# One encoder layer on one core: all queues issued in the sequence of one list schedule

## The chip, the cores and the metric

The kernel runs on one core of a Trainium2 chip. The core has a matrix engine (TensorE, PE in the profile, with its weight loads as PEld), VectorE (DVE), ScalarE (ACT), GpSimd (POOL), SyncE (SP), which here only issues transfers, and DMA queues that move data between device memory and the on-chip memory. Each engine works through its own queue of instructions; an instruction that needs something of another queue waits for a semaphore. Matmuls write to PSUM, here eight tiles of 128x512 fp32, four named `mm` and four named `ax`.

The metric is device time in microseconds, the median of several executions. One more execution was taken with the hardware profiler on; every row of a profile in this document comes from such an execution.

## The reference

One layer of a hybrid encoder, sequence 512, width 1024, batch 1, all in fp32:

```python
h = _rmsnorm(x, norm_mix[i])
proj = h @ w_in[i]                                   # 768 q-latent | 256 kv-latent | 32 rope key | 3 x 512 Hyena
c_q, c_kv, k_pe, u_h = proj[..., :c1], proj[..., c1:c2], proj[..., c2:c3], proj[..., c3:]
q  = (_rmsnorm(c_q, q_norm[i]) @ w_uq[i])            # 8 heads x 96
kv = (_rmsnorm(c_kv, kv_norm[i]) @ w_ukv[i])         # 8 heads x (64 key + 64 value)
# q, k: rmsnorm per head, rotary on the last 32; softmax attention over 512 keys
y_attn = _block_attention(q, k, v)
u_h = _dwconv3(u_h, short_conv_w[i], short_conv_b[i]); x0, x1, vh = jnp.split(u_h, 3, axis=-1)
h_fwd, h_bwd = _hyena_filters(...)                   # three sine layers
y_hyena = x0 * _bidir_long_conv(x1 * vh, h_fwd, h_bwd, hyena_bias[i])   # FFT convolution
x = x + concat(_rmsnorm(y_attn), _rmsnorm(y_hyena)) @ w_out[i]
up = _dwconv3(_rmsnorm(x, norm_ffn[i]) @ w_up[i], ffn_conv_w[i], ffn_conv_b[i])
x = x + (jax.nn.silu(up[..., :D_FF]) * up[..., D_FF:]) @ w_down[i]      # D_FF = 2816
x = x + jax.nn.sigmoid(x @ w_ple_gate[i]) * _rmsnorm(p[i] @ w_ple[i], ple_norm[i])
```

## The kernel before

Everything is held transposed: a tile is 128 channels by 512 positions. Every fp32 operand of a large product is split into a high and a low part of a shorter format (`split`, lines 129 to 135), and each product of a 128x128 weight block with a 128x512 tile is three matmuls: high times high, high times low, low times high (`prod3`, line 181). A group of such matmuls that sums into one PSUM tile (8 blocks, 24 matmuls, for a 1024-deep product) is called a chain here.

Weights come as a stream of 115 tiles (`stream`, lines 149 to 156). `wload` (lines 137 to 147) loads one into `wr` (two buffers), writes the high part `wh` on ACT (line 142; three buffers) and the low part `wl` on DVE (line 143; three buffers); for the tiles of the first stages half of `wl` is made by ACT and an adding transfer on POOL's queue (lines 145, 146).

The stages, in the order in which TensorE takes them:

- The input projection, 21 weight tiles (`in_gemm`): first the two kv tiles together, then the rope key, twelve Hyena tiles and six q tiles. The sum of squares of x goes through `rms_bcast` (lines 218 to 222: a matmul with a tile of ones, then logarithm and exponential on ACT and two steps on DVE) into `R1`, by which each result is multiplied when it leaves PSUM. Between its matmuls, tasks of the filter network, the Fourier transforms and the spectral product are woven in (`spawn`, `advance`, with delays in constants such as `D_FILT`).
- Keys, queries, values, head norms and the inverse transforms. `query_scale` (line 674) sums squares with a ones matmul, copies the rows (`rows`, line 667, ACT), turns them by small transposes (`turn_rows`, line 231). `key_task` (lines 686 on) does the same for the keys, spreads the result (line 698 to 705, `t8`, `selT`), scales the keys, and calls `prep`, which moves one head's query and key rows by four transfers (lines 745, 746) and splits them (747, 748).
- Attention, head by head: scores (three matmuls on a 96-row operand), softmax (lines 864 to 869: maximum on DVE, exponential on ACT, division on POOL or DVE), turning of the probabilities (line 941), weighing (`weigh`), with the gates of the Hyena branch and the first part of the output projection between them.
- The output projection, then the up projection (44 tiles; each result goes through DVE line 1059, ACT 536, DVE 537 and 543, then SiLU, product and split), the down projection (eight chains of 66 matmuls, three weight tiles each), and the gate (eight tiles).

What sets the order: TensorE's queue follows the program's text (`manual_schedule(engines={PE})`). The other queues are sequenced by the framework's own scheduler, which the kernel steers by priorities (`high_priority` with offsets in `PRI`, `WPRI`, `CPRI`). Of the first head's four transfers all are issued from ACT's queue (`QACT = 1`), of the others from SP's.

Of the kernel before, what the change touches and what calls it, by code (L numbers as in the profile page):

```python
# [12 lines left out]
F32 = mybir.dt.float32  # L13
# [49 lines left out]
CPRI = 50  # L63
EPS = 1e-6
NH = 8
NFF = 22
# [17 lines left out]


@with_exitstack
def tile_encoder_block(
# [5 lines left out]
    nc = tc.nc  # L93
    V, S, G, PE, SP = nc.vector, nc.scalar, nc.gpsimd, nc.tensor, nc.sync

# [6 lines left out]
    def pri(key):  # L102
        return tc.high_priority(offset=PRI[key]) if PRI.get(key) else nullcontext()

    ctx.enter_context(tc.manual_schedule(engines={mybir.EngineType.PE}))
    const = ctx.enter_context(tc.tile_pool(name="const", bufs=1))
    apool = ctx.enter_context(tc.tile_pool(name="apool", bufs=16))
    wpool = ctx.enter_context(tc.tile_pool(name="wpool", bufs=2))
    gpool = ctx.enter_context(tc.tile_pool(name="gpool", bufs=20))
    xpool = ctx.enter_context(tc.tile_pool(name="xpool", bufs=8))  # L110
    psm = ctx.enter_context(tc.tile_pool(name="psm", bufs=4, space=PSUM))
    psx = ctx.enter_context(tc.tile_pool(name="psx", bufs=4, space=PSUM))

# [128 lines left out]

    def act_table(name):
        tc.keep_in_program_order(S.preload_act_table_set(name))

    act_table("natural_log_exp_and_others")


    p2 = ExitStack()
    hp = p2.enter_context(tc.tile_pool(name="hp", bufs=1))  # L250
    gp = p2.enter_context(tc.tile_pool(name="gp", bufs=1))
    p0 = ExitStack()
    ft = p0.enter_context(tc.tile_pool(name="ft", bufs=1, reuse_waits="tile"))

# [241 lines left out]
    rms_bcast(R1, accx, 1024, tmp, "x")  # L496
    SP.dma_start(rope, c_rope)
    SP.dma_start(ident, c_id)
    with tc.issue_after(gate_consts.ins):
# [6 lines left out]
        G.memset(f32(t8), 0.0)  # L506
    ckv = [xpool.tile([P, T], F32, tag="x", name="x") for _ in range(2)]
    for i in range(2):
# [141 lines left out]

    act_table("natural_log_exp_and_others")

# [79 lines left out]
    def prep(h, pool=None):  # L732
        j, i, g4, i4 = h // 2, h % 2, h // 4, h % 4
        raws = None if pool else {nm: atile(F32)[0:96, :] for nm in "qk"}
        for nm, src in (("q", qt), ("k", kt_)):
            if pool is None:
                raw = raws[nm]
                a, b = (atile()[0:96, :] for _ in range(2))
            else:
                raw = pool.tile([P, T], F32, tag=f"{nm}r", name=f"{nm}r")[0:96, :]  # L740
                ab = pool.tile([P, 2, T], F32R, tag=f"{nm}s", name=f"{nm}s")
                a, b = ab[0:96, 0, :], ab[0:96, 1, :]
            with tc.high_priority(offset=CPRI if h < 2 else 0):
# [148 lines left out]
    Rh = const.tile([P, T], F32, tag="R1", name="Rh")  # L892
    p0.close()


    p1 = ExitStack()
    at = p1.enter_context(tc.tile_pool(name="at", bufs=1, reuse_waits="tile"))

# [11 lines left out]
    Ra = at.tile([P, T], F32, tag="Ra", name="Ra")  # L910
    ap_ = p1.enter_context(tc.tile_pool(name="ap", bufs=1, reuse_waits="tile"))

# [89 lines left out]
    while fill < 8:  # L1002
        if fill == 8 - RFILL:
            with tc.high_priority(offset=RPRI):
                rms_bcast(Ra, acc5, 512, tmp1, "a")
# [32 lines left out]
    rms_bcast(R2, acc6, 1024, tmp1, "f")  # L1038
    p1.close()
    p2.close()  # L1040


    fp = ctx.enter_context(tc.tile_pool(name="fp", bufs=1, reuse_waits="tile"))

# [69 lines left out]
    for m in range(8):  # L1114
# [5 lines left out]
        if m == 0:  # L1120
            act_table("natural_log_exp_and_others")
# [177 lines left out]
```

## Time and profile before

| | us |
|---|---|
| median of 3 runs | 759.44 (757.58 to 759.54) |
| profiled execution, device time | 757.62 |
| its span, first to last instruction | 755.8 |
| TensorE busy | 723.0 |
| VectorE busy | 504.8 |
| ScalarE busy | 373.1 |
| GpSimd busy | 151.7 |

A row of a timeline gives start and duration in us, engine, line, operation, output<-inputs, sizes and how many equal instructions were merged; in brackets stands the idle time of the engine before it and what ended it. `PE` rows of merged matmuls overlap, so the distance between starts is the rate. A row of the windows gives, for one stretch, its length and then the busy time of each engine with its number of instructions, the granted TensorE clock as a share, the share of the DMA engines and GB/s. A row of waits gives who waited for whom, the total in us, how often, and the longest.

### The profile page before, as it was taken

The page shows a single profiled execution, that of the slowest core. Times are in us where ns is not written, and L with a number is a line of the kernel's source. Part 1 is how long each engine was busy: PE and PEld are TensorE (multiplying, and loading weights), DVE is VectorE, ACT ScalarE, POOL GpSimd, SP SyncE. Part 2 cuts the span into 40 slices and gives each one's busy share as a digit, 9 for nine tenths or more (in the row PEclk, how much of TensorE's full clock was granted, in tenths as well). Part 3 has the DMA queues.
Part 4 walks back from the last instruction along what each step waited for, and adds up shares of the span by engine and source line. Part 5 has one row for each costly group of instructions (what it writes and reads, how often), then busy time and mean ns, then how long its engine had stood idle before and what let it go on. Part 6 is the DMA issues. An engine that isn't in the chain of part 4 may idle for free.

```text
span 755.8 us, 9037 instructions
## 1 busy us (share of the span) xinstructions
PE 723.0 (96%) x3254; PEld 582.7 (77%) x3254; DVE 504.8 (67%) x780; ACT 373.1 (49%) x575; POOL 151.7 (20%) x150
## 2 busy tenths in 40 slices
PE   6999999996997899999999999999999999999997
PEld 4767888874665777788888888888888888888886
DVE  6499988888779987885766566666665332233482
ACT  7465545467668896564534444444353222126340
POOL 2111101110126662130422222222122000005000
PEclk9999999997999999999999999999999999999999
DMA  8765744443636210533232323232323233323331
GB/s 279 239 153 128 191 128 91 106 94 77 147 91 170 71 25 19 126 103 106 83 113 84 112 84 112 83 104 92 106 89 92 82 109 101 98 90 127 111 112 56
DMA packets 30110, 82.83 MB, mean 110 GB/s; under 512 B 3913, under 2 KB 5257, under 8 KB 30066
## 3 DMA queue, kind: packets, MB, share of 16 engines
q1 hardware_dynamic: 24418, 71.62, 31.2%
q0 software_dynamic: 5392, 10.25, 7.2%
q10 hardware_dynamic: 256, 0.39, 0.2%
q8 instruction: 25, 0.41, 0.2%
q14 instruction: 19, 0.16, 0.1%
HBM read 77.00 MB, written 2.10 MB: 105 GB/s over the span
## 4 chain that ended last, share of the span: by engine, by line
PE 54%; DVE 0%; ACT 0%; DVEq 0%; issue 0%
PE mm L176 37%; PE ax L176 17%; PE ax L220 0%; DVE t L1127 0%; ACT t L1126 0%; DVEq L1294 0%; DVE t L1128 0%
## 5 line engine op out<-in xcount | busy, mean ns | idle before, releaser
L176 PE MATMUL mm<-a,wh 128*128 128x512 f32 (+1 forms) x928 | 288.8, 392 | 9.2 <-ACT wh L273 6.4
L176 PEld LDWEIGHTS mm<-a,wh 128*128 128x128 f32 x928 | 174.3, 190 | 51.2 <-issue 6.5
L143 DVE TENSOR_TENSOR wl<-wr,wh 128x1024 fp32r<-128x1024 f32 (+3 forms) x113 | 124.3, 1101 | 113.8 <-ACT wh L142 111.8
L142 ACT ACTIVATE wh<-wr 128x1024 fp32r<-128x1024 f32 (+1 forms) x113 | 116.5, 1031 | 158.0 <-PE mm L176 121.6
L176 PE MATMUL mm<-a,wl 128*128 128x512 f32 (+1 forms) x464 | 180.7, 389 | 0.0
L176 PE MATMUL ax<-a,wh 128*128 128x512 f32 x384 | 118.3, 389 | 0.0
L176 PEld LDWEIGHTS mm<-a,wl 128*128 128x128 f32 x464 | 88.1, 190 | 17.8 <-DVE wl L274 0.2
L176 PEld LDWEIGHTS ax<-a,wh 128*128 128x128 f32 x384 | 72.1, 188 | 14.9
L176 PE MATMUL mm<-g,wh 128*128 128x512 f32 x232 | 73.8, 400 | 1.7 <-ACT t L647 1.7
L176 PE MATMUL ax<-a,wl 128*128 128x512 f32 x192 | 74.7, 389 | 0.0
L1063 POOL TENSOR_TENSOR f<-f 128x512 f32<-128x512 f32 x22 | 28.7, 1303 | 169.2 <-DVE f L543 149.5
L176 PE MATMUL mm<-h,wh 128*128 128x512 f32 x192 | 59.0, 389 | 0.0
L176 PEld LDWEIGHTS mm<-g,wh 128*128 128x128 f32 x232 | 44.2, 192 | 13.7 <-ACT t L647 2.1
L176 PE MATMUL mm<-g,wl 128*128 128x512 f32 x116 | 46.1, 397 | 0.0
L176 PEld LDWEIGHTS ax<-a,wl 128*128 128x128 f32 x192 | 36.0, 188 | 7.6
L176 PEld LDWEIGHTS mm<-h,wh 128*128 128x128 f32 x192 | 36.0, 188 | 7.5
L1059 DVE TENSOR_TENSOR f<-mm,R 128x512 f32<-128x512 f32 x22 | 15.2, 691 | 33.7 <-PE mm L176 33.7
L176 PE MATMUL mm<-h,wl 128*128 128x512 f32 x96 | 37.3, 389 | 0.0
L1062 ACT ACTIVATE f<-f 128x512 f32<-128x512 f32 x22 | 13.9, 631 | 44.8 <-DVE f L543 44.8
L536 ACT ACTIVATE f<-f,par 128x512 f32<-128x512 f32 x44 | 35.5, 808 | 1.0 <-DVE f L1059 1.0
L543 DVE SCALAR_TENSOR_TENSOR f<-f,par 128x511 f32<-128x511 f32 x44 | 33.9, 771 | 1.4
L146 POOL DMA_DIRECT2D wl<-in_w_in_dram x16 | 13.9, 868 | 103.8 <-DVE wl L143 53.5
(312 smaller groups left out, 1015.1 us busy)
## 6 DMA issues: line engine op xcount, KB each, us to landing
wr<-in_w_up_dram SPq DMA_DIRECT2D x44, 512.0 KB, 3.5
wr<-in_w_in_dram SPq DMA_DIRECT2D x19, 512.0 KB, 3.9
wr<-in_w_down_dram SPq DMA_DIRECT2D x16, 512.0 KB, 3.5
x<-in_xT_dram SPq DMA_DIRECT2D x16, 256.0 KB, 4.2
wl<-in_w_in_dram POOLq DMA_DIRECT2D x16, 256.0 KB, 5.3
wr<-in_w_out_dram SPq DMA_DIRECT2D x8, 512.0 KB, 4.4
wr<-in_w_gate_dram SPq DMA_DIRECT2D x8, 512.0 KB, 3.6
wr<-in_w_down_dram SPq DMA_DIRECT2D x8, 384.0 KB, 3.1
```

The lines of the kernel that those rows point to most:

```text
L142: S.activation(hi[:, :n], raw[:, :n], AF.Copy)
L143: V.tensor_tensor(lo[:, :cut], raw[:, :cut], f32(hi[:, :cut]), op=ALU.subtract)
L146: G.dma_start(lo[:, cut:n], src[:, cut:n], accum_op=ALU.add)
L176: last = PE.matmul(out, l, r, start=start and i == 0, stop=stop and i == n - 1)
L536: S.activation(c, z, AF.Identity, scale=pcol(w, 3 * m + 1), bias=pcol(b, m))
L543: V.scalar_tensor_tensor(c[:, 0 : T - 1], z[:, 1:T], pcol(w, 3 * m + 2), c[:, 0 : T - 1], op0=ALU.mult, op1=ALU.add)
L1059: V.tensor_tensor(z, ps_up.pop(m), R2, op=ALU.mult)
L1062: S.activation(cc[0], cc[0], AF.Silu)
L1063: G.tensor_tensor(cc[1], cc[0], cc[1], op=ALU.mult)
```

## The change

The kernel's text now calls recorders in place of the engines. Each call is kept as an operation with the parts of tiles that it reads and writes; from these follow its predecessors. Tiles are planned too: a pool's tag has numbered slots, taken in the program's order. `cost` gives each operation a duration and a latency by formulas of its engine and size. `order` gives TensorE's operations due times by the program's text (backward over the graph for everything else, and over TensorE's chains too), and then takes operations one after the other: for each engine the one that can start first, and of those within 0.02 of it the one that is due first. TensorE takes part in this, so its order may leave that of the text as well. `issue` emits the operations in that sequence, and the framework schedules nothing (`manual_schedule(engines=None)`). The priorities go away, and `QACT` is 0, so that the first head's four transfers are issued from SP's queue like those of the other heads. What is computed, and which engine computes it, stays.

```diff
-QACT = 1
+QACT = 0
...
+    def record(self, eng, fn, args, kw):
...
+        for views, write in ((ins, False), (outs, True)):
+            for v in views:
...
+                for other, obox, owrite in t.log:
+                    if other is not op and (write or owrite):
+                        if box[0] <= obox[1] and obox[0] <= box[1] and box[2] <= obox[3] and obox[2] <= box[3]:
+                            op.preds.add(other)
...
+    def cost(self, op):
...
+            else:
+                op.dur = (n + 32) / 2400.0
+            op.lat = 0.25
...
+    def order(self):
+        clock = 5.5
+        for op in self.ops:
+            if op.eng == "PE":
+                op.due = clock
+                clock += op.dur
+            else:
+                op.due = None
+            for p in op.preds:
+                p.succs.append(op)
+        for op in reversed(self.ops):
+            need = clock + 50.0 if op.due is None else op.due
+            for s in op.succs:
+                need = min(need, s.due - op.dur - op.lat - AIM - (2.0 + op.byte / 2.0e5 if op.byte else 0.0))
+            op.due = need
...
+                    for op in cand:
+                        t = max(op.est, engines[e])
+                        if op.port:
+                            t = max(t, port["G" if e == "V" else "V"])
...
+                    now = min(t for t, _ in fit)
+                    t, op = min(((t, op) for t, op in fit if t <= now + 0.02), key=lambda x: (x[1].due, x[1].i))
+                    if best is None or t < best[0]:
+                        best = (t, op)
...
+                engines[op.eng] = t + dur
+                op.end = t + dur + op.lat
...
+    def issue(self):
...
+        for _, op in self.order():
...
+            getattr(self.handles[op.eng], op.fn)(*[real(v) for v in op.args], **{k: real(v) for k, v in op.kw.items()})
...
-    V, S, G, PE, SP = nc.vector, nc.scalar, nc.gpsimd, nc.tensor, nc.sync
+    plan = Plan(tc, {"V": nc.vector, "S": nc.scalar, "G": nc.gpsimd, "PE": nc.tensor, "SP": nc.sync})
+    V, S, G, PE, SP = (plan.engine(k) for k in ("V", "S", "G", "PE", "SP"))
...
-    ctx.enter_context(tc.manual_schedule(engines={mybir.EngineType.PE}))
...
+    ctx.enter_context(tc.manual_schedule(engines=None))
...
-            with tc.high_priority(offset=WPRI if len(ready) > 3 else 0):
+            with nullcontext():
                 ready.append(wload(*stream[len(ready)]))
...
+    plan.issue()
```

Three places show what moves. In the rows `mm` and `ax` are PSUM tiles, `a` and `g` split activations, `wh` and `wl` the two parts of a weight tile; the last number of a name tells tiles apart, and in the changed kernel the number before it is the slot. All rows of the changed kernel have the line of `issue`.

TensorE near the start, before: the ones matmul that begins the first norm (`accx`) stands behind the whole chain of the third weight tile (`wh_203`, the rope key), that is behind 72 matmuls.

```order
L176 MATMUL mm_288<-a_160,wh_203 128x512
L176 MATMUL mm_288<-a_159,wl_204 128x512
L220 MATMUL ax_313<-accx_182,ones_81 128x512
L176 MATMUL mm_353<-a_125,wh_209 128x512
L176 MATMUL mm_353<-a_126,wh_209 128x512
```

TensorE at the same place in the changed kernel:

```order
L441 MATMUL mm_1_158<-a_15_234,wh_1_151 128x512
L441 MATMUL mm_1_158<-a_14_214,wl_1_160 128x512
L441 MATMUL ax_0_259<-accx_0_108,ones_0_88 128x512
L441 MATMUL mm_2_265<-a_0_113,wh_2_250 128x512
L441 MATMUL mm_2_265<-a_1_120,wh_2_250 128x512
```

It now stands right behind the two kv chains, 48 matmuls from the start; the rope key's chain (`mm_2_265`) follows it.

TensorE at the queries' scale, before: the four small transposes of the copied rows (`ident_80,t_1627`) stand directly behind those of `R1`.

```order
L176 MATMUL mm_1647<-g_1324,wh_1562 128x512
L176 MATMUL mm_1647<-g_1323,wl_1563 128x512
L231 MATMUL ax_1662<-ident_80,R1_189 128x8 x4
L231 MATMUL ax_1668<-ident_80,t_1627 128x8 x4
L690 MATMUL ax_1440<-qr_185,ones_81 8x512
L176 MATMUL mm_1647<-g_1375,wh_1562 128x512
```

TensorE at the same transposes (`t_9_1691`) in the changed kernel:

```order
L441 MATMUL mm_0_1598<-g_13_1445,wh_1_1530 128x512
L441 MATMUL mm_1_1653<-g_1_1289,wh_2_1567 128x512
L441 MATMUL mm_0_1598<-g_16_1427,wl_1_1540 128x512
L441 MATMUL ax_1_1696<-ident_0_238,t_9_1691 128x8 x4
L441 MATMUL mm_1_1653<-g_6_1277,wl_2_1573 128x512
L441 MATMUL mm_1_1653<-g_8_1350,wh_2_1567 128x512
```

Between the ones matmul of the queries' sum and these transposes stand 16 matmuls on 512 columns before, and the transposes of `R1`; in the changed kernel 46 matmuls on 512 columns, and the transposes of `R1` are spread among them.

TensorE in the up projection, before: one chain of 24 after the other, each on its own weight tile.

```order
L176 MATMUL ax_4051<-a_3344,wh_3967 128x512
L176 MATMUL ax_4051<-a_3343,wl_3968 128x512
L176 MATMUL mm_4094<-a_3177,wh_4010 128x512
L176 MATMUL mm_4094<-a_3178,wh_4010 128x512
L176 MATMUL mm_4094<-a_3177,wl_4011 128x512
```

TensorE in the up projection in the changed kernel:

```order
L441 MATMUL mm_3_3964<-a_7_3312,wh_2_3928 128x512
L441 MATMUL ax_0_4006<-a_9_3218,wh_0_3966 128x512
L441 MATMUL mm_3_3964<-a_6_3324,wh_2_3928 128x512
L441 MATMUL ax_0_4006<-a_10_3203,wl_0_3977 128x512
L441 MATMUL mm_3_3964<-a_7_3312,wl_2_3937 128x512
L441 MATMUL ax_0_4006<-a_11_3222,wh_0_3966 128x512
```

Two chains are open at a time nearly everywhere and take turns, matmul by matmul, so two of the three weight slots are in use together. Between the last matmul on a slot's old `wh` and the first on its new one stood 49 other matmuls before; now it is 25 in the up projection, and at nine places of the down projection and the last gate tile only 7. Further up, from the key scales' transposes (`ks`, line 698) to the first matmul that spreads them (`selT`, line 705), stood 24 matmuls on 512 columns before and stand four now. TensorE's queue changes its PSUM tile about 2,600 times in the changed kernel, and some 290 times before.

More of the change, by code (lines that the diff above doesn't have):

```diff
@@ L83, with _axes, _rearrange @@
 PI_LO = 3.1415925
+def _axes(side):
+    out, group = [], None
+    for w in side.replace("(", " ( ").replace(")", " ) ").split():
+        if w == "(":
+            group = []
+        elif w == ")":
+            out.append(group)
+            group = None
+        elif group is None:
+            out.append([w])
+        else:
+            group.append(w)
+    return out
+def _rearrange(idx, pattern, sizes):
+    left, right = (_axes(s) for s in pattern.split("->"))
+    size = dict(sizes)
+    for n, group in zip(idx.shape, left):
+        known = 1
+        for w in group:
+            known *= size.get(w, 1)
+        for w in group:
+            if w not in size:
+                size[w] = n // known
+    flat = [w for g in left for w in g]
+    idx = idx.reshape([size[w] for w in flat])
+    idx = idx.transpose([flat.index(w) for g in right for w in g])
+    shape = []
+    for g in right:
+        n = 1
+        for w in g:
+            n *= size[w]
+        shape.append(n)
+    return idx.reshape(shape)
@@ new lines, with __init__, shape, __getitem__ @@
+class View:
+    def __init__(self, tile, idx, steps, dtype):
+        self.tile, self.idx, self.steps, self.dtype = tile, idx, steps, dtype
+        self._box = None
+    @property
+    def shape(self):
+        return self.idx.shape
+    def __getitem__(self, key):
+        return View(self.tile, self.idx[key], self.steps + (("get", key),), self.dtype)
+    def rearrange(self, pattern, **sizes):
+        return View(self.tile, _rearrange(self.idx, pattern, sizes), self.steps + (("re", pattern, sizes),), self.dtype)
+    def bitcast(self, dtype):
+        return View(self.tile, self.idx, self.steps + (("cast", dtype),), dtype)
+    def box(self):
+        if self._box is None:
+            n = self.tile.width
+            row = self.idx[0]
+            self._box = (int(self.idx.min()) // n, int(self.idx.max()) // n, int(row.min()) % n, int(row.max()) % n)
+        return self._box
+    def real(self):
+        ap = self.tile.real
+        for s in self.steps:
+            if s[0] == "get":
+                ap = ap[s[1]]
+            elif s[0] == "re":
+                ap = ap.rearrange(s[1], **s[2])
+            else:
+                ap = ap.bitcast(s[1])
+        return ap
@@ new lines, with __init__, open_slots, view @@
+class Slot:
+    def __init__(self, pool, tag, n):
+        self.pool, self.tag, self.n = pool, tag, n
+        self.free = 0.0
+class Tag:
+    def __init__(self, pool, name, bufs):
+        self.pool, self.name, self.bufs = pool, name, bufs
+        self.tiles, self.next, self.slots = [], 0, None
+    def open_slots(self):
+        if self.slots is None:
+            self.slots = [Slot(self.pool, self, n) for n in range(min(self.bufs, len(self.tiles)))]
+        return self.slots
+class PlannedTile:
+    def __init__(self, tag, shape, dtype):
+        self.tag, self.shape, self.dtype = tag, tuple(shape), dtype
+        self.width = 1
+        for n in shape[1:]:
+            self.width *= n
+        self.slot, self.left, self.first, self.end, self.real = None, 0, None, 0.0, None
+        self.log = []
+    def view(self):
+        return View(self, np.arange(self.shape[0] * self.width, dtype=np.int32).reshape(self.shape), (), self.dtype)
@@ new lines, with __init__, tile @@
+class PlanPool:
+    def __init__(self, plan, name, bufs, kw):
+        self.plan, self.name, self.bufs, self.kw = plan, name, bufs, kw
+        self.first, self.last, self.tags = len(plan.cuts), None, {}
+        self.psum = kw.get("space") == PSUM
+        plan.pools.append(self)
+    def tile(self, shape, dtype, tag, name=None, bufs=None):
+        t = self.tags.get(tag)
+        if t is None:
+            t = self.tags[tag] = Tag(self, tag, bufs or self.bufs)
+        return PlannedTile(t, shape, dtype).view()
@@ new lines, with __init__, __getattr__ @@
+class Op:
+    __slots__ = ("i", "eng", "fn", "args", "kw", "acc", "seg", "preds", "succs", "dur", "lat", "due", "wait", "est", "new", "end", "table", "byte", "port")
+class Recorder:
+    def __init__(self, plan, eng, handle):
+        self._plan, self._eng, self._handle = plan, eng, handle
+    def __getattr__(self, fn):
+        return lambda *args, **kw: self._plan.record(self._eng, fn, args, kw)
+TABLES = {AF.Ln: "exp", AF.Exp: "exp", AF.Sin: "sin", AF.Silu: "silu", AF.Sigmoid: "sigmoid"}
@@ L241, in rms_cols @@
             rsqrt(out, v, col(), ps, n, "c")
[L243 to L253, printed above, removed]
+    nc.scalar.preload_act_table_set("natural_log_exp_and_others")
+    hp = plan.pool("hp", 1)
+    gp = plan.pool("gp", 1)
+    ft = plan.pool("ft", 1, reuse_waits="tile")
     def tmp(dt=F32):
@@ L496, in tile_encoder_block @@
     rms_bcast(R1, accx, 1024, tmp, "x")
-    SP.dma_start(rope, c_rope)
-    SP.dma_start(ident, c_id)
-    with tc.issue_after(gate_consts.ins):
+    plan.behind = gate_consts
+    if True:
+        SP.dma_start(rope, c_rope)
+        SP.dma_start(ident, c_id)
         for i in (0, 1):
@@ L506, in tile_encoder_block @@
         G.memset(f32(t8), 0.0)
+    plan.behind = None
     ckv = [xpool.tile([P, T], F32, tag="x", name="x") for _ in range(2)]
```

214 lines of the change are left out of this document (195 added, 19 removed).

## The prediction

> **What bounds the kernel now.** I first read the stretches, cut where the PE waits below end.
>
> ```profile
> span 755.8 us, 9037 instructions
> 0.00:40.00 40.00, 31.24 (x113) 23.71 (x114) 22.81 (x33) 23.80 (x36) 7.54 (x16) 0.96 0.82 256
> 40.00:150.00 110.00, 109.11 (x477) 87.39 (x477) 99.01 (x169) 55.73 (x81) 12.97 (x15) 1.00 0.54 133
> 150.00:214.60 64.60, 56.33 (x227) 38.31 (x225) 50.75 (x96) 42.66 (x79) 7.79 (x9) 0.92 0.47 111
> 214.60:300.00 85.40, 75.77 (x442) 61.68 (x442) 76.09 (x178) 67.84 (x144) 46.28 (x51) 1.00 0.28 69
> 340.20:751.20 411.00, 410.84 (x1830) 340.29 (x1830) 219.68 (x255) 159.61 (x203) 67.81 (x51) 1.00 0.31 98
> ```
>
> From 340 to 751 us TensorE is never idle, and the other engines are at half load or less: nothing is to be had there, only lost. The chain of waits says the same, matmuls one behind the other, and nothing else, up to 751 us:
>
> ```profile
> 352.78 5.44 PE ax L176 x24
> ...
> 712.69 38.42 PE mm L176 x192
> ```
>
> A matmul on 512 columns costs 5.44/24 = 0.227 us. All that the change can win lies before 340 us, in PE's waits:
>
> ```profile
> PE ax L231 <- ACT t L667: 6.5, 2, 5.8
> PE mm L176 <- ACT wh L273: 6.4, 1, 6.4
> PE ax L176 <- DVE ptl L132: 3.2, 2, 2.9
> PE mm L176 <- DVE x L509: 1.9, 1, 1.9
> PE mm L176 <- ACT t L647: 1.7, 1, 1.7
> PE mm L176 <- DVE ptl L132: 1.5, 5, 0.4
> PE ax L941 <- DVE st L865: 1.4, 1, 1.4
> PE ax L176 <- ACT pr L867: 1.1, 1, 1.1
> ...
> PE ax L370 <- ACT x L377: 0.9, 1, 0.9
> ```
>
> Two of them cost more than their length, because the matmuls behind them run at half rate:
>
> ```profile
> 34.96 0.70 PE L176 MATMUL mm<-a,wh 128*128 128x512 f32 x2 [1.86 <-DVE x L509]
> 36.33 0.63 PE L176 MATMUL mm<-a,wl 128*128 128x512 f32 x1
> 39.32 0.66 PE L176 MATMUL mm<-a,wh 128*128 128x512 f32 x2
> 171.08 1.02 PE L674 MATMUL ax<-accx,ones 128*8 128x512 f32 x2
> 182.01 0.59 PE L231 MATMUL ax<-ident,t 8*128 8x8 f32 x4 [5.79 <-ACT t L667]
> 184.33 1.22 PE L176 MATMUL mm<-g,wh 128*128 128x512 f32 x2
> 189.19 0.58 PE L176 MATMUL mm<-g,wl 128*128 128x512 f32 x1
> ```
>
> Seven matmuls start from 36.33 to 39.32, 2.99 us instead of 7 x 0.227 = 1.59: 1.4 us lost. Eleven start from 184.33 to 189.19, 4.86 us instead of 2.50: 2.4 us lost. The granted clock of that stretch above is 0.92. The Trainium skill, "TensorE: Matmul & The Clock Gate", section "HAM oscillation — how this bites in real kernels", has the array slow down after gaps of more than about 3.4 us. The first row disagrees, since 1.86 us were enough here; by the page the second term below would be 1.9 instead of 3.3 and the sum 1.4 less.
>
> **The change, part by part.** The sum is made on the profiled execution, 757.62 us, of which 1.8 lie around the span; the median of the three runs is 1.8 above it.
>
> *Start.* PE's first 6.4 us wait for the first `wh`, and that for its weights:
>
> ```profile
> 1.19 0.42 SPq L283 DMA_DIRECT2D gm<-in_g_mix_dram  x1
> 1.65 0.43 SPq L269 DMA_DIRECT2D wr<-in_w_in_dram  x1
> 5.74 0.63 ACT L273 ACTIVATE wh<-wr 128x512 fp32r<-128x512 f32 x1 [1.01 <-DMA wr<-in_w_in_dram]
> ```
>
> The weights are now issued ahead of the gains, 0.46 us earlier. The gains feed the activation before, which has 1.01 us to spare. Gain 0.4 (0 to 0.46).
>
> *First norm.* Its ones matmul moves from behind 72 matmuls to behind 48, so the norm's steps start 24 x 0.227 = 5.4 us earlier against the stream. The kv results leave PSUM before the chain that waited 1.86 us for their tile; only if the steps became 3.5 us longer would it wait again. The wait and the half rate behind it go: 1.9 + 1.4 = 3.3 (0 to 3.3).
>
> *Sine layer and q chains.* The waits on L377 (0.9) and L647 (1.7) stand where PE's order now has another open chain. I take 0.9 and 1.2, since the second hangs on a PSUM tile and chains now hold theirs twice as long: 2.1 (0 to 2.6).
>
> *Query scale.* The rows' way from the ones matmul (171.08) to the transposes (182.01) takes 10.9 us. Beside it lay 16 matmuls; now 46, or 10.4 us. Wait and half rate (5.8 + 2.4, rounded 8.2, and about 0.8 on the fp32 matmuls between them: 184.33 - 182.01, less 0.5 for the transposes, less the 1.02 that such a pair takes at 171.08) make 9.0; I leave 1.0 for a remainder: 8.0. If ACT reaches the rows 3 us later than now, 3 us of wait come back, with some half rate: low end 3.
>
> *Key scale.* Here the new order loses cover. Before, from the transposes to the spreading, ACT and DVE made `t8` while PE had 24 matmuls:
>
> ```profile
> 192.89 0.60 PE L698 MATMUL ax<-ident,ks 128*8 128x128 f32 x4
> 195.42 0.68 DVE L701 TENSOR_TENSOR t<-ax,t 8x512 fp32r<-8x512 f32 x1 [0.18 <-ACT t L700]
> ```
>
> From 192.89 to the end at 196.10 are 3.2 us, of which the transposes take 0.4. Now four matmuls, 0.9 us, stand there: a wait of about 1.9 appears (1.5 to 4, if DVE comes to it late). Minus 1.9. The first head's transfers now stand in SP's queue, where weight loads wait for free buffers; the scores stand some 7 us of matmuls behind the last spreading, so I cost it at nothing (up to 3 if a load ahead of them waits).
>
> *Attention.* The waits on `ptl`, `st` and `pr` add to 3.2 + 1.5 + 1.4 + 1.1 = 7.2 us. DVE is busy 76.1 of 85.4 us, so no order wins all of it: at 95% DVE load, higher than in any stretch above, the stretch would be 80.1, 5.3 less. Some of that load is itself a wait:
>
> ```profile
> L135 DVE SCALAR_TENSOR_TENSOR a<-x,par,a x12: 737/766/2945, 234.1 to 338.4; 128x512 fp32r<-128x512 f32 x12
> 235.25 1.26 POOL L842 TENSOR_TENSOR x<-x,t 128x512 f32<-128x512 f32 x1
> ```
>
> The first row gives shortest, median and longest of twelve like instructions in ns; the longest, 2.9 instead of 0.8 us, begins at 234.1 and ends at 237.1, just after the POOL instruction's end at 236.5. The new cost rules keep such two apart in the plan, though nothing holds them apart on the chip. I take 3.5 (minus 2 to 7).
>
> *Weights.* With two chains open the slot of a `wh` must be refilled sooner. What a refill takes:
>
> ```profile
> 466.63 0.39 PE L176 MATMUL ax<-a,wl 128*128 128x512 f32 x1
> 466.83 1.06 ACT L142 ACTIVATE wh<-wr 128x1024 fp32r<-128x1024 f32 x1 [0.39 <-PE ax L176]
> 467.93 1.23 DVE L143 TENSOR_TENSOR wl<-wr,wh 128x1024 fp32r<-128x1024 f32 x1
> ```
>
> The slot's last matmul started one step before 466.63, at 466.40; `wh` was ready at 467.89, 1.5 us later, `wl` at 469.16. The up projection gives 26 x 0.227 = 5.9 us, so 4.4 stay free. The nine tight places give 8 x 0.227 = 1.8 us, 0.3 more than needed, if ACT is free. ACT has 39% load there (160 of 411), and an instruction ahead costs at most about 0.6. I take nine times 0.1: minus 0.9 (0 to minus 6).
>
> *Taking turns between PSUM tiles.* The kv chains do it already, every three matmuls; then one of them runs alone:
>
> ```profile
> 13.49 0.63 PE L176 MATMUL mm<-a,wh 128*128 128x512 f32 x2
> 14.18 0.63 PE L176 MATMUL mm<-a,wh 128*128 128x512 f32 x2
> 19.80 0.62 PE L176 MATMUL mm<-a,wh 128*128 128x512 f32 x2
> 20.49 0.62 PE L176 MATMUL mm<-a,wh 128*128 128x512 f32 x2
> ```
>
> Three matmuls take 0.69 us both ways, so the roughly 2,300 further changes cost nothing. A price below 0.01 per change would not show here; it is kept as a part of the slower case.
>
> Sum: 0.4 + 3.3 + 2.1 + 8.0 - 1.9 + 3.5 - 0.9 = 14.5 us less, 743.1. **Predicted: 743.** Check against DVE: before the scores it is busy 22.8 + 99.0 + 50.8 = 172.6 of 214.6 us; with the first five terms (11.9) it is 172.6 of 202.7, 85% — tight over the middle stretches, but possible.
>
> **The rivals.**
> *Fuller cover.* Every wait before 340 us goes: 0.4 + 3.3 + 2.6 + 9.0 + 7.2 = 22.5, and the key scale is hidden by DVE being early: 735. For it speaks that the list fills PE with whatever is ready; against it DVE's 76 of 85 us.
> *DVE takes it back.* From 40 to 150 us DVE is at 99 of 110, and PE now asks for its results earlier. Then the start and the first norm stay (3.7), the query scale gives its low end (3), attention and the rest nothing, key scale and weights cost 2.8: about 4 less, 754. Against it: DVE's load falls to 51 of 65 just where the largest wait is.
> *Slower: weights come late.* Two chains hold two of three slots through the 78 weight tiles from the up projection on. Should each refill stand behind other work on ACT or DVE so that PE waits for every tile, it decides from 14.5/78 = 0.19 us per tile. At 0.4 us per tile it is 31 - 14.5, some 17 slower: 774. A change between PSUM tiles at 14.5/2300 = 6 ns would weigh the same. For it: the window halves from 50 to 26 matmuls. Against it: 4.4 us are free in 44 of the 78.
> *It changes nothing.* PE's queue is full from 340 us, and before that a sequence made from formulas could fall out of step at the first late transfer (DMA share 0.82 to 40 us), so that each wait moves but none goes: 758.
>
> **How the numbers follow.** 743 as summed 0.52, fuller cover 0.10, DVE takes it back 0.15, slower 0.15, nothing 0.08. The likeliest case's own range is 737 to 752: on the fast side all its best ends (0.46 + 3.3 + 2.6 + 9.0 - 1.5 + 7 = 20.9 less), on the slow side a third of the way to all its worst ends (3 - 4 - 3 - 2 - 6, 12 more than now), which have separate causes. The range of 732 to 758 adds the fuller cover and DVE's case, and leaves out the slower one. About 0.3% (2.3 us) is what a measurement of this kernel tells from no change: faster 0.52 + 0.10 + 0.15 = 0.77, within it 0.08, slower 0.15.
>
> **What would show it.** First `wh` wait 6.0 instead of 6.4; no wait on the kv results near 33 us and no half rate behind it; no wait over 2 us at the queries' transposes, but about 2 us ahead of the first spreading matmul; scores that begin near 203 instead of 214.6; attention of about 82 us; from the up projection on 411 us of matmuls as before, with waits on `wh` below 1 us in all. I am wrong if PE shows waits on `wh` or `wl` at many tiles there, if a step of 24 matmuls takes more than 5.46 us with no wait, or if DVE's waits before 214 us move to PE.

## The result, and the profile after

| | before | changed |
|---|---|---|
| median of four runs each, us | 758.75 | 747.54 |
| lowest to highest | 757.58 to 759.54 | 746.65 to 748.96 |
| profiled execution | 757.62 | 746.80 |
| its span | 755.8 | 745.0 |
| TensorE busy | 723.0 | 721.5 |

The ratio is 0.9855, with a 95% interval of 0.9831 to 0.9879: the change is 1.45% faster. The forecast was 743.1 for the profiled execution; 746.8 was measured, 10.8 us less than before where 14.5 were forecast.

The stretches of the changed kernel, in the columns used before (start and end, length, then busy time and number of instructions of PE, PEld, DVE, ACT and POOL, granted clock, DMA share, GB/s). The cuts stand where the same work begins:

```profile
0.00:40.00 40.00, 32.60 (x124) 24.57 (x124) 26.72 (x40) 25.55 (x39) 7.33 (x16) 1.00 0.71 234
40.00:150.00 110.00, 110.00 (x487) 89.45 (x486) 97.95 (x166) 54.81 (x80) 14.54 (x17) 1.00 0.56 141
150.00:212.20 62.20, 57.77 (x224) 37.50 (x222) 50.60 (x99) 43.47 (x81) 6.90 (x8) 0.92 0.53 126
212.20:284.80 72.60, 66.72 (x403) 53.97 (x401) 67.94 (x167) 63.69 (x137) 46.72 (x51) 1.00 0.28 73
335.00:740.50 405.50, 404.26 (x1802) 334.28 (x1800) 229.69 (x253) 158.19 (x202) 83.13 (x51) 1.00 0.30 97
```

TensorE has no idle time left from 40 to 150 us, attention (fourth row) is done in 72.6 us, and from 335 us on TensorE is idle for 1.2 of 405.5 us. The third row still has 4.4 idle us and the same low mean clock, 0.92, as the kernel before. What TensorE waits for (who for whom, total, how often, longest):

```profile
PE mm L441 <- ACT wh L441: 7.0, 1, 7.0
PE mm L441 <- ACT g L441: 3.0, 1, 3.0
PE ax L441 <- DVE ptl L441: 2.8, 2, 1.7
PE ax L441 <- ACT pr L441: 1.4, 3, 0.5
PE ax L441 <- DVE t L441: 1.3, 1, 1.3
PE ax L441 <- DVE pl L441: 1.0, 1, 1.0
```

The 5.8 us at the queries' transposes and the 1.9 us on the kv results are gone. New is a wait of 3.0 us on `g`, and 1.3 us on `t`, the low part of `t8`. Both stand in the key scale. TensorE's timeline there:

```profile
187.06 1.58 PE L441 MATMUL mm<-a,dft 128*128 128x512 f32 x6
191.65 0.73 PE L441 MATMUL mm<-a,dft 128*128 128x512 f32 x2 [3.02 <-ACT g L441]
192.22 0.60 PE L441 MATMUL ax<-ident,ks 128*8 128x128 f32 x4
192.58 1.18 PE L441 MATMUL mm<-a,dft 128*128 128x512 f32 x4
195.05 0.50 PE L441 MATMUL ax<-t,selT 40*128 40x512 f32 x1 [1.29 <-DVE t L441]
...
197.52 1.87 PE L441 MATMUL ax<-t,sel 128*8 128x512 f32 x4
...
203.36 1.05 PE L441 MATMUL mm<-a,dft 128*128 128x512 f32 x2
```

Four `sel` matmuls start from 197.52 to 199.32, 1.80 us where four take 0.91. The windows of the same place show it as the clock (columns as above):

```profile
188.00:192.00 4.00, 0.98 (x5) 0.48 (x3) 3.75 (x11) 3.94 (x10) 0.00 (x0) 1.00 0.22 49
192.00:196.00 4.00, 2.71 (x13) 1.30 (x11) 3.35 (x7) 3.65 (x8) 1.00 (x2) 1.00 0.52 82
196.00:208.00 12.00, 12.00 (x30) 5.48 (x30) 6.53 (x13) 4.25 (x9) 0.73 (x1) 0.57 0.50 103
```

The first row also shows ACT at 3.94 of 4 us while TensorE stands still. In the third the clock is 0.57: 12 x 0.43 = 5.1 us lost, more than the waits ahead of it.

To set the forecast's terms against the two traces I took, for every TensorE matmul, the distance to the next start less its undisturbed time (0.227 us for 512 columns, 0.45 for each of the fp32 ones and filter matmuls, 0.30 for `selT`, 0.117, 0.11 and 0.07 for 256, 128 and 8 columns), and summed it by stage. These are TensorE's lost microseconds, waits and slow clock together:

| stage (cuts before / after) | before | after | gained | forecast |
|---|---|---|---|---|
| until the first matmul | 6.4 | 7.0 | -0.6 | +0.4 |
| to 40: first norm | 7.6 | 3.8 | +3.8 | +3.3 |
| 40 to 150: sine layer | 2.3 | 0.8 | +1.5 | +0.9 |
| 150 to the last query chain (189.7 / 187.1): q chains, query scale | 12.0 | 2.9 | +9.1 | +9.2 |
| to the first scores (214.7 / 212.2): key scale | 3.1 | 10.7 | -7.6 | -1.9 |
| to the last turned probabilities (295.3 / 284.8): attention | 15.3 | 11.0 | +4.3 | +3.5 |
| the rest: weights | 2.1 | 1.8 | +0.3 | -0.9 |
| sum | 48.9 | 38.0 | +10.8 | +14.5 |

One term is far off, the key scale, by 5.7 us. The others together came out 2.0 us better than forecast.

### The profile page after: what moved, and what is told of

Read it like the earlier page. It is cut to its first block, busy times and chain, and to the rows that moved or that the text cites. A ratio compares the mean times of both kernels' runs of the same rounds, so it can differ in the third digit from the quotient of the medians.

```text
span 745.0 us, 9047 instructions
## 1 busy us (share of the span) xinstructions
PE 721.5 (97%) x3254; PEld 580.8 (78%) x3254; DVE 513.6 (69%) x780; ACT 372.1 (50%) x575; POOL 168.4 (23%) x150
## 4 chain that ended last, share of the span: by engine, by line
PE 88%; DVE 5%; ACT 4%; issue 1%; DMA 1%; SPq 0%; DVEq 0%; ACTq 0%
PE mm L441 62%; PE ax L441 26%; DVE st L441 2%; DVE t L441 1%; ACT pr L441 1%; ACT a L441 1%; DMA gm<-in_g_mix_dram 1%; ACT t L441 1%; DVE ptl L441 1%; ACT pth L441 0%; ACT wh L441 0%; DVE wl L441 0%; DVE g L441 0%; DVE x L441 0%; ACT accy L441 0%
## 5 line engine op out<-in xcount | busy, mean ns | idle before, releaser
L441 PE MATMUL mm<-a,wh 128*128 128x512 f32 (+1 forms) x928 | 312.5, 391 | 7.0 <-ACT wh L441 7.0
L441 ACT ACTIVATE wh<-wr 128x1024 fp32r<-128x1024 f32 (+2 forms) x117 | 118.7, 1016 | 199.7 <-PE mm L441 186.1
L441 PE MATMUL mm<-a,wl 128*128 128x512 f32 (+1 forms) x464 | 171.7, 390 | 0.0
L441 PE MATMUL ax<-a,wh 128*128 128x512 f32 x384 | 147.9, 389 | 0.0
L441 DVE SCALAR_TENSOR_TENSOR f<-f,par,f 128x511 f32<-128x511 f32 x88 | 86.3, 982 | 3.0 <-ACT f L441 1.5
L441 PE MATMUL mm<-g,wh 128*128 128x512 f32 x232 | 78.6, 393 | 0.0
L441 PE MATMUL mm<-h,wh 128*128 128x512 f32 x192 | 66.6, 389 | 0.0
L441 POOL TENSOR_TENSOR f<-f,f 128x512 f32<-128x512 f32 x22 | 29.3, 1331 | 143.6 <-DVE f L441 143.6
L441 POOL TENSOR_TENSOR acc<-acc,t 128x512 f32<-128x512 f32 x13 | 19.0, 1465 | 116.4 <-ACT t L441 116.2
L441 PE MATMUL mm<-g,wl 128*128 128x512 f32 x116 | 44.6, 393 | 0.0
```

The costliest lines, as they stand in the source:

```text
L441: getattr(self.handles[op.eng], op.fn)(*[real(v) for v in op.args], **{k: real(v) for k, v in op.kw.items()})
```

## The experiments

Eleven runs. Ratios are to the kernel before on the same chip, with the 95% interval.

### Whose order gains: TensorE in the program's text

```diff
+        text = [op for op in self.ops if op.eng == "PE"]
...
-                    for op in cand:
+                    for op in [o for o in cand if o is text[0]] if e == "PE" and text else cand:
...
+                if op.eng == "PE":
+                    text.pop(0)
```

> The changed kernel, but TensorE may take an operation only when all TensorE operations ahead of it in the program's text are taken; the other queues are still sequenced by the list. Theory A (the prediction's): most of the gain is cover that TensorE's new order puts beside the norms, so text order gives it back: the wait at the queries' transposes is above 3 us again, the time 754 to 760. Rival B: the gain is that ACT, DVE and POOL do the urgent operation first, whatever TensorE's order: 745 to 750, and the wait at the queries' transposes below 2 us.

Measured: 770.14 us, ratio 1.0157 (1.0139 to 1.0175), slower than the kernel before. The waits of this run:

```profile
PE mm L444 <- ACT pth L444: 8.6, 2, 7.9
PE ax L444 <- ACT t L444: 6.2, 2, 5.5
PE ax L444 <- DVE qs L444: 4.9, 1, 4.9
```

The wait at the queries' transposes (`t`, 5.5) is back, as theory A said, and two more have come: 4.9 in the key scale and 7.9 in attention (`pth` and `ptl` are the two parts of the turned probabilities). The time is 10 us above A's range, so it is more than A: with TensorE held to the text, the list's sequence of the other queues, with its tile slots and the first head's transfers on SP, is 11.5 us worse than the framework's own. TensorE's freedom is worth 22.6 us to this list (770.1 to 747.5), the whole gain and more. The opposite pairing, TensorE's new order with the other queues left to the framework, was not run, so what the new order alone would be worth stays open.

### Where in the program: text order from the first scores on

```diff
+                    for op in [o for o in cand if o.i < self.scores or o is text[0]] if e == "PE" and text else cand:
```

> The changed kernel, but TensorE keeps the order of the program's text from the first scores on; ahead of them its order is the list's, and the other queues are the list's everywhere. From the first scores to the last turned probabilities the kernel before took 80.5 us, the change 72.5. Theory A: attention gained by TensorE taking whichever head's operation is ready, so the stretch is 80 us or more and the time 754 to 760. Rival B: it gained by the sequence of DVE's and ACT's work: below 76 us, 746 to 750.

Measured: 757.83 us, ratio 0.9999 (0.9978 to 1.0020). From the first scores (205.3) to the last turned probabilities (291.4) it took 86.1 us, 72.5 in the change; the scores begin 6.9 us sooner here, so that some work which stood ahead of them in the change now lies in the stretch. By the table's measure attention loses 20.0 us instead of 11.0, and the stages behind it, also in text order, about 1 us more than in the change. (The profiled execution took 753.67 us, 4 less than the median.) Two of its waits:

```profile
PE mm L444 <- DVE ptl L444: 6.3, 11, 1.1
PE ax L444 <- POOL x L444: 2.5, 1, 2.5
```

Eleven short waits on `ptl`, where the change has two: TensorE, held to the text, stands behind one head's probabilities. That work of another head was ready meanwhile is argued. Theory A holds.

### Not the port rule

```diff
-            op.port = n > 64 and len(ins) > 1 and not any(v.tile.tag.pool.psum for v in ins)
+            op.port = False
...
-            op.port = n > 64 and op.fn != "memset"
+            op.port = False
```

> The changed kernel without the rule that keeps large DVE and POOL operations apart in the plan. Theory A: the attention stretch (72 us from the first scores to the last turned probabilities, where the kernel before took 81) gained because the rule keeps DVE from running beside POOL: without it single DVE operations of 2 to 3 us are back, and the stretch takes 4 to 8 us longer, 751 to 756. Rival B: the stretch gained by the sequence of DVE's and ACT's work alone: within 2 us of the changed kernel, 746 to 749.

Measured: 747.64 us, ratio 0.9863 (0.9826 to 0.9900), against 0.9855 for the change. Rival B: the rule that keeps DVE and POOL apart carries none of the gain that this many runs can tell. In its profile the stretch takes 73.9 us, and the longest DVE operation in it 1.8 us, 1.7 in the change and 2.9 before: the operations of 2 to 3 us do not come back without the rule. The executions lie between 745.6 and 751.6, so 2 us either way stay open.

### Interleaved chains, everywhere and in one place

Without the latency between two TensorE operations the due times no longer alternate between chains:

```diff
-                need = min(need, s.due - op.dur - op.lat - AIM - (2.0 + op.byte / 2.0e5 if op.byte else 0.0))
+                need = min(need, s.due - op.dur - (0.0 if s.eng == op.eng == "PE" else op.lat) - AIM - (2.0 + op.byte / 2.0e5 if op.byte else 0.0))
```

> The changed kernel, but the latency of 0.25 us no longer counts between two TensorE operations when due times are made, so that chains are no longer interleaved matmul by matmul; everything else is as in the change. Theory A (the prediction's): taking turns between PSUM tiles and the halved refill window cost next to nothing, so from 340 us on the matmuls run at 0.227 us each with no wait on wh or wl in both kernels, and the time differs only by what happens before 300 us; without the interleaving a chain ends in half the time and the work after it starts sooner, so the key scale's cover is larger: 742 to 748. Rival B: interleaving is what fills TensorE in the first 300 us, and without it the waits before 214 us come back: 750 to 757.

Measured: 738.64 us, ratio 0.9739 (0.9709 to 0.9769), 9 us better than the change and 3 us below theory A's own range. By the table's measure its key scale loses 3.8 us instead of 10.7. Then the same for the six query chains alone:

```diff
-                need = min(need, s.due - op.dur - op.lat - AIM - (2.0 + op.byte / 2.0e5 if op.byte else 0.0))
+                need = min(need, s.due - op.dur - (0.0 if op.flat and s.eng == "PE" else op.lat) - AIM - (2.0 + op.byte / 2.0e5 if op.byte else 0.0))
...
         for k in range(0, 6, 2):
+            plan.flat = True
             mms(ps, prod3(w[k : k + 2], zq[k : k + 2]), start=k == 0, stop=k == 4)
+            plan.flat = False
```

> The changed kernel, but only in the six query chains does the latency no longer count between TensorE operations, so only these are not interleaved matmul by matmul. All chains at once gave 738.6. Theory A: the loss sits at the query chains: two interleaved chains end together, their results come to ACT at once (it is busy 3.94 of 4 us from 188 to 192 us), and the wait of 3.0 us on g at 188 us is for a PSUM tile that ACT has not emptied; then this edit alone gives 737 to 742, with a wait there below 1 us and no low clock behind it. Rival B: it sits elsewhere (the kv, Hyena or filter chains, or attention): 745 to 749, with the wait as in the change.

Measured: 740.11 us, ratio 0.9761 (0.9748 to 0.9774): 7.4 of the 9 us lie at these six chains, and the clock from 196 to 208 us is 1.00 as theory A said. The waits of the two runs on `g`, first all chains, then the query chains alone:

```profile
PE mm L441 <- ACT g L441: 0.7, 1, 0.7
```

```profile
PE mm L443 <- ACT g L443: 0.7, 1, 0.7
```

The wait of 3.0 us fell to 0.7 in both. It ends in the change, and without any interleaving, with these ACT operations, each the second pass over a query chain's tile:

```profile
190.92 0.68 ACT L441 ACTIVATE g<-mm,par 128x512 f32<-128x512 f32 x1
```

```profile
188.62 0.68 ACT L441 ACTIVATE g<-mm,par 128x512 f32<-128x512 f32 x1
```

The tile comes free 2.3 us earlier, and TensorE's waiting matmul starts 2.3 us earlier (191.65 and 189.35). By the sequence of issue and the starts, the last matmul of the third to the fifth query chain starts 1.2 to 1.7 us later when they share TensorE with the next one (175.2, 179.3 and 184.3 instead of 173.5, 178.1 and 182.8), and that of the sixth at the same time (186.8 and 186.9). ACT's queue shows where this reaches it: it stands before the split of a weight tile, whose `wh` buffer the third query chain still reads. In the change, and without any interleaving:

```profile
175.16 0.85 ACT L441 ACTIVATE wh<-wr 128x768 fp32r<-128x768 f32 x1 [2.01 <-PE mm L441]
```

```profile
173.68 0.85 ACT L441 ACTIVATE wh<-wr 128x768 fp32r<-128x768 f32 x1 [0.94 <-PE mm L441]
```

The last matmul on that buffer starts at 174.7 us in the change and at 173.3 without interleaving. The windows of the two from 172 to 189 us:

```profile
172.00:189.00 17.00, 16.64 (x72) 11.92 (x72) 12.06 (x24) 14.16 (x27) 1.72 (x2) 1.00 0.42 99
```

```profile
172.00:189.00 17.00, 16.63 (x75) 12.80 (x74) 13.85 (x30) 15.87 (x31) 1.73 (x2) 1.00 0.46 100
```

ACT works 14.16 of the 17 us in the change and 15.87 without interleaving, so 1.7 of the 2.3 us by which it empties the tile later are time in which it stands still ahead of it, most of them before such buffers (2.01 + 0.38 against 0.94). With the query chains alone untied it works 14.36 us and takes the tile at 190.11, only 0.8 us sooner than in the change; there TensorE has the key scales' transposes ahead of the waiting matmul and comes to it at 190.1 instead of 188.6. That the loss sits at these chains is shown by both runs; that ACT's stand before the weight buffers is how it comes about rests on this one pair of traces. Rival B of both runs falls.

### Is it the clock: filler

```diff
+        turned_k = turn_rows(k)
+        plan.behind = plan.ops[-1]
+        warm = ax_ps()
+        for n in range(32):
+            PE.matmul(warm, ck[0][0][:, 0:P], ck[0][0], start=True, stop=True)
+        plan.behind = None
```

> The changed kernel with 32 more matmuls of 128x512 that compute nothing of use (their PSUM tile is never read); they may start when the keys' rows are turned, at about 184 us, and take 7.3 us. In the changed kernel TensorE waits 3.0 and 1.3 us between 188 and 195 us, and from 196 to 208 us its granted clock is 0.57, worth 5.1 us. Theory A: the low clock comes from these two waits; work that fills them keeps it at 1.0, so that 4.3 + 5.1 = 9.4 us go and 7.3 come: 744 to 747. Rival B: the slow stretch has another cause (the operands, PSUM, the other engines): the filler hides at most the 4.3 us of waits and costs 3 on top, 749 to 752, with a clock below 0.7 from 196 to 208 us as before.

Measured: 745.75 us, ratio 0.9829 (0.9810 to 0.9848). TensorE's work is 7.3 us longer and the program is not slower (1.8 us faster, which the two intervals do not separate). The windows of this run at the same place:

```profile
188.00:192.00 4.00, 4.00 (x22) 3.20 (x21) 3.21 (x12) 1.95 (x5) 0.00 (x0) 1.00 0.07 16
196.00:208.00 12.00, 12.00 (x48) 7.00 (x48) 9.98 (x22) 7.85 (x15) 0.96 (x2) 1.00 0.72 142
```

No idle time, and the clock stays at 1.00 from 196 to 208 us, where it was 0.57: 48 matmuls in the 12 us instead of 30. The low clock comes from the waits (theory A): of the 10.7 us that the key scale loses in the change, 4.3 are waits and 5.1 the clock behind them. (The 5.1 is clock time. By the starts, the matmuls from the first spreading one to the first scores take 17.14 us in the change and the same ones 12.48 without interleaving, at full clock: 4.7 us.) The filler does not put work into the holes themselves: it ran from 183.2 to 190.6 us and thereby kept query chains back for later.

### A tile or the data: an earlier due time for the reader of a PSUM tile

```diff
+            for t in {x[0] for x in op.acc if x[0].tag.name in ('mm',)}:
+                n = t.tag.tiles.index(t) + t.tag.bufs
+                if n < len(t.tag.tiles) and t.tag.tiles[n].first.i > op.i:
+                    need = min(need, t.tag.tiles[n].first.due - op.dur - op.lat)
```

> The changed kernel (chains interleaved), with one more rule for due times: the last reader of an mm tile is due before the first matmul that needs the same tile again. In the change TensorE waits 3.0 us on g at 188 us and 1.3 us on t before the first spreading matmul. Theory A: the 3.0 us are a wait for a PSUM tile that ACT empties late; with this rule ACT empties it first, the wait on g falls below 1 us, but the keys' rows come no sooner, so the wait before the spreading grows to 3.5 to 5 us and the time stays within 2 us of the change, 745.5 to 749.5. Rival B: the wait on g is for data, and stays at 3 us. Rival C: the tile alone was the loss, the wait does not come back and the time falls below 743.

Measured: 748.48 us, ratio 0.9864 (0.9832 to 0.9895), the change's within its uncertainty. The place in its timeline:

```profile
190.20 3.32 PE L445 MATMUL mm<-a,dft 128*128 128x512 f32 x12
194.80 0.60 PE L445 MATMUL ax<-ident,ks 128*8 128x128 f32 x4 [1.27 <-DVE col L445]
197.56 0.49 PE L445 MATMUL ax<-t,selT 40*128 40x512 f32 x1 [2.17 <-DVE t L445]
```

and its window from 192 to 196 us, where TensorE is idle and DVE and ACT are full:

```profile
192.00:196.00 4.00, 2.12 (x10) 1.19 (x10) 3.75 (x13) 3.97 (x10) 0.58 (x1) 1.00 0.29 66
```

All twelve transform matmuls now run through: the 3.0 us were a wait for a PSUM tile. Then TensorE waits 1.27 + 2.17 = 3.44 us on the keys' rows, just under the 3.5 that theory A asked for, and from 196 to 208 us the clock is 0.60. Theory A in the main; the profile also has a wait of 2.2 us for a weight transfer near 57 us, which the change has not, so the equal times are no exact balance. Emptying the tile sooner only shows what is late next, the rows; what pays is to have matmuls left over for this place.

### The first norm alone, in the kernel before

```diff
-    pe_ps = in_gemm(2)
     rms_bcast(R1, accx, 1024, tmp, "x")
+    pe_ps = in_gemm(2)
```

> The kernel before with one edit: the ones matmul of the first norm stands behind the two kv chains (48 matmuls) instead of behind the rope key's chain (72). Theory A (the prediction's second term): the 1.9 us wait on the kv results near 33 us and the half-rate matmuls behind it go, worth 3.3 us, so 0.4% faster than before, 755 to 756 where before is near 758.7. Rival B: the norm's result is not early enough or ACT and DVE do something else first, and the wait moves behind the ones matmul: within 1 us of before.

Measured: 759.94 us, ratio 1.0026 (1.0014 to 1.0038): slightly slower. Two of its waits:

```profile
PE mm L176 <- ACT wh L273: 5.4, 1, 5.4
PE ax L370 <- ACT x L377: 3.6, 1, 3.6
```

The first is the start, 5.4 us here and 6.4 before, so this profile even began sooner. The wait on the kv results is gone and with it the slow matmuls (the first 40 us lose 4.7 instead of 7.6), but the wait of the sine layer on L377 has grown from 0.9 to 3.6 us, with a slow stretch behind it (40 to 150 us lose 7.7 instead of 2.3). Theory A falls; neither theory named that place, and 1.8 us slower is more than rival B's 1 us. The change has no wait of the sine layer; in the order of the kernel before the term of 3.3 us is not to be had alone.

### The start

On top of the run without interleaving, the gains' transfer first:

```diff
-            op.due = need
+            op.due = 0.0 if op.byte and op.acc[0][0].tag.name == "gm" else need
```

> No interleaving of chains anywhere (738.6), and the gains' transfer is issued first, as in the kernel before. Theory A: in the change the first product waits on the gains, which are now issued behind the first weights and arrive last; issued first, the first matmul starts at 6.0 to 6.4 us instead of 6.6 to 7.0, and the time is 737.5 to 738.5. Rival B: the start is set by when the first transfers happen to land; the runs so far start anywhere from 5.9 to 7.0 with the same order, and this one does too, 738 to 739.

Measured: 736.45 us, ratio 0.9723 (0.9698 to 0.9748). In its profile the first matmul starts at 7.41 us, later than in any other run, though the gains went first. What ACT waited for at the start, in the changed kernel and then in this run:

```profile
5.72 0.72 ACT L441 ACTIVATE a<-x,gm 128x512 fp32r<-128x512 f32 x1 [1.75 <-DMA gm<-in_g_mix_dram]
```

```profile
4.17 0.72 ACT L441 ACTIVATE a<-x,gm 128x512 fp32r<-128x512 f32 x1 [2.15 <-DMA x<-in_xT_dram]
6.73 0.63 ACT L441 ACTIVATE wh<-wr 128x512 fp32r<-128x512 f32 x1 [1.31 <-DMA wr<-in_w_in_dram]
```

Once the gains land last, once the weights. Theory A's earlier start falls, and this one profile fits rival B: when the first transfers land decides more than half a microsecond of their order. The time lies below both ranges but differs from 738.64 by less than either run's spread, so nothing follows from it.

### Better due times, worse durations

On top of the last, ten constants that set the text's order, and so the due times (here three of them):

```diff
-UQ = (2, 0, 4, 3, 5, 1)
-D_KS = 5.0
-D_SIN = 8.0
+UQ = (2, 0, 4, 3, 1, 5)
+D_KS = 3.4
+D_SIN = 4.8
```

> No interleaving, the gains first, and ten weaving constants of the program's text moved (the order of the six query chains and the delays of the filter, sine and key tasks), which set TensorE's due times. The waits of TensorE in the list's own sequence fall from 11.7 to 8.3 us. Theory A: the chip follows the list, so 3 us of that arrive: 731 to 735. Rival B: transfers and the clock decide what is left, and it ends within 1.5 us of the run without the moved constants (736.45): 735 to 738.

Measured: 732.71 us, ratio 0.9663 (0.9639 to 0.9686), theory A. This is the fastest version, 2.0% ahead of the change (0.9663 against 0.9855). Its waits after the start, the longest three:

```profile
PE mm L441 <- ACT pth L441: 1.5, 2, 1.1
PE mm L441 <- DVE ptl L441: 0.8, 1, 0.8
PE ax L441 <- DVE ptl L441: 0.7, 1, 0.7
```

The key scale has no wait on `g` or `t8` left and loses 1.7 us. And, on the run without interleaving, a duration that is wrong:

```diff
-STRETCH = {'V': 1.0, 'S': 1.0, 'G': 1.0, 'PE': 1.0, 'SP': 1.0}
+STRETCH = {'V': 1.1, 'S': 1.0, 'G': 1.0, 'PE': 1.0, 'SP': 1.0}
```

> No interleaving (738.6), but the list counts each DVE operation 10% too long. Theory A: the list's durations matter because it takes whichever operation it believes can start first: DVE is the fullest of the helpers before 275 us, so a wrong duration puts TensorE's operations in a worse order; 743 to 748. Rival B: the sequence hardly hangs on durations of this size: 737 to 741.

Measured: 743.72 us, ratio 0.9797 (0.9768 to 0.9827): 5.1 us lost (4.4 by the ratios), theory A. The loss shows in attention, 16.9 lost us instead of 8.5, of them one long wait:

```profile
PE mm L441 <- ACT pth L441: 5.2, 3, 4.3
```

## Why the prediction was right, and where it was not

*Direction and size.* The time fell where it was expected to, before 340 us, and 747.5 lies in the range and in the likeliest case's own (737 to 752). The sum was 3.7 us too hopeful, and that is one term.

*Key scale: the step that failed.* The text said: "Now four matmuls, 0.9 us, stand there: a wait of about 1.9 appears", minus 1.9. Measured: minus 7.6. Two things were missing. First, it looked at the rows' chain alone. The transform matmuls that it counted as work ahead need a PSUM tile, and ACT, at 3.94 of 4 us, had not emptied one: 3.0 us of wait beside the 1.3 on `t8`. That the interleaving of the query chains brings it is shown by the run that unties just these six (the wait falls to 0.7 and the time by 7.4 us, the low clock being part of it). The text priced weight buffers that are held longer only from the up projection on; here ACT stood 2.0 us before one, ahead of that tile. Second, it priced half rate behind the two waits that the kernel before had, and none behind the one that it said would come. That is 5.1 us, shown by the filler, which takes the waits away and the low clock with them.

*Query scale and q chains: right.* 8.0 and the 1.2 for L647 were forecast, 9.1 measured. That TensorE's own order carries it is shown by the text-order run, in which 5.5 us of wait are back.

*First norm: right in the change, 3.8 for 3.3, but the step was incomplete.* It named no next late work. There is one: moved alone, the norm gives way to the sine layer's wait. In the change that wait does not occur; that it is because the sine layer moved with the norm is argued.

*Attention: right size, 4.3 for 3.5, wrong reason.* The text took DVE's load as the limit, and the load came out near it: 67.9 of 72.6 us, 94%, where 95% was taken. But DVE's work was not the same: from the first scores to the last turned probabilities it fell from 73.9 to 67.8 us. And the text counted on the rule that keeps DVE and POOL apart, and without the rule the time is the same. What brings DVE to that load is TensorE's order, since with TensorE in text order the gain is gone. Part of the shorter stretch, 80.5 to 72.5 us, is work that now stands elsewhere: 8.0 shorter, of which 4.3 are lost time.

*Weights: no cost where they were priced.* From 335 us on no row of the waits names `wh` or `wl`; the only wait there is 1.0 us on `pl` near the gate. Minus 0.9 was forecast, and the slower rival with 0.4 us per tile does not occur.

*Taking turns between PSUM tiles: right by itself, wrong in its consequence.* The chain of waits has

```profile
571.19 97.07 PE mm L441 x428
```

or 0.2268 us per matmul, interleaved, the same 0.227 as before. A change of tile costs nothing. But what the interleaving does to the time of the results cost 7.4 us at the query chains, and no step or rival had that.

*Start: wrong sign, small.* 7.0 us instead of the 6.0 forecast, against 6.4. The gains' transfer had 1.0 us to spare in the one trace that the step used; in the changed kernel's it was the last to land.

*The signs to look for.* Scores were to begin near 203 us and began at 212.2: the key scale's 5.7 us, and work of about 4 us that now stands ahead of the scores (lost time before the scores fell by 6.2 us, their start by 2.5).

## What to carry to other kernels

A list schedule that takes whatever can start spends its independent matmuls early; count what is left as cover where the next serial chain (a norm's rows) comes, and price the low clock behind every wait that you forecast, not only behind those that the trace shows. Interleaving two accumulations costs nothing per matmul, but it moves their results later and holds their weight buffers longer, and the engine that refills these buffers and empties PSUM comes late to both; let chains end one after the other unless the second would wait. Before crediting an order of helper queues, run it with TensorE's order held: here nothing of the gain was left without TensorE's freedom.

## What the runs showed of the hardware

The same waits need not bring the same clock. Without interleaving, the profiles with and without the gains first have identical waits at the key scale, 0.71 and 1.28 us ahead of the same matmuls. The windows of the first and of the second:

```profile
196.00:208.00 12.00, 12.00 (x54) 8.61 (x53) 10.44 (x24) 5.59 (x15) 0.00 (x0) 1.00 0.58 152
```

```profile
196.00:208.00 12.00, 12.00 (x39) 6.32 (x38) 7.93 (x19) 5.48 (x13) 0.00 (x0) 0.72 0.55 119
```

The clock is 1.00 in one and 0.72 in the other: 3.4 us of clock time, and by the starts 2.9 us (from the first spreading matmul to the first scores 15.36 us instead of 12.48). With and without the gains first, the executions above 739 us are those with a mean clock of 0.992 or 0.993, and the ones below 738 have 0.998 or 0.999, so the time goes with the clock; where it falls in those without a profile is not shown.

The traces record two clocks only, full and half. Apart from the start and the end of the program, every stretch at half clock in all thirteen traces lasts 3.41 us or two or three times that: 3.41 from 36.0 us and 10.24 from 179.3 in the kernel before, 10.24 in the change, 6.83 in the second run above. The windows of these last two:

```profile
196.76:207.00 10.24, 10.24 (x22) 4.31 (x22) 5.15 (x10) 3.28 (x6) 0.00 (x0) 0.50 0.51 102
```

```profile
195.77:202.60 6.83, 6.83 (x15) 2.18 (x14) 4.79 (x9) 2.18 (x4) 0.00 (x0) 0.50 0.44 94
```

The Trainium skill, "TensorE: Matmul & The Clock Gate", section "What's actually happening", has the clock follow activity in a free-running window of about 3.4 us. These lengths agree, and that equal waits can fall differently into such a window agrees with the first two rows. The same section has the clock fall after an idle window of about 3.4 us. That does not agree: here 2.0 us of waiting within 4.1 us were enough, and in the changed kernel 3.0 and 1.3.

The clock also falls late and stays low for long. In the changed kernel the matmuls behind the 3.0 us wait still run at full rate at 192.6 us; the low stretch begins at 196.8, 5.1 us after that wait, and ends at 207.0.
